# Tanh gates multiplied on VectorE, and low weight parts summed by an accumulating DMA

## The chip, the cores and the metric

The kernel runs on one NeuronCore of one Trainium2 chip. Its measure is the device time of one execution in microseconds: 2702.65 us before the change, the median of three runs (2695.49 to 2704.43).

## The reference

Two decoder layers over 1024 tokens of width 1024, in float32. A layer normalizes x and projects it by one matrix of 4352 columns into queries (16 heads of 64), keys and values (2 heads each), the convolution's value u and gate ug (512 channels each), and two output gates of 1024 channels.

```python
def conformer_conv(u, ug, w_dw, b_dw, ln_g, ln_b, w_pw):
    a = u * jax.nn.sigmoid(ug)
    y = ...causal depthwise convolution of width 31 over a, plus b_dw
    y = jax.nn.silu(layernorm(y, ln_g, ln_b))
    return y @ w_pw

h = rmsnorm(x, norm_mix[l])
q, k, v, u, ug, ga, gb = jnp.split(h @ w_in[l], SPLITS, axis=-1)
a_out = sliding_window_attention(q, k, v, sinks[l])    # QK-norm, partial rotary, window 128
c_out = conformer_conv(u, ug, ...)
merged = jax.nn.sigmoid(ga) * a_out + jax.nn.sigmoid(gb) * c_out
x = x + merged @ w_out[l]
h2 = rmsnorm(x, norm_ffn[l]); g, up = jnp.split(h2 @ w_gate_up[l], 2, axis=-1)
x = x + (jax.nn.silu(g) * up) @ w_down[l]
```

## The kernel before

Tensors lie with channels on the 128 partitions and tokens along the free axis. A float32 product is built of three matmuls: each operand is split into a high part rounded to fp32r and a low part, what is left, and high by high, high by low and low by high are summed in PSUM (`mm3`, L236).

**Weights.** `fetch` (L120) keeps a short queue of weight tiles of 128x1024. SyncE loads a tile into `raw` (L125), ScalarE rounds it into `wh` (L133), GpSimd subtracts to get `wl` (L134). There are two buffers each of `raw` and `wl` and three of `wh`, so `wl` of one tile is written while TensorE still reads that of the tile before, once TensorE has let go of the tile before that one.

**The attention stage.** After keys and values each layer runs 30 more input projections (`project`, L758; two more follow after the stage), each of eight steps of six 512-column matmuls (`dense`, L257). Between the steps TensorE does 32 attention units of two heads' two blocks each: scores `S` (`unit_s`, L625), transposes `pT` (`unit_t`), masks on GpSimd (`masks`, L678: four affine selects, `mo` twice, then `ph` and `pl` in place) and the product with the values, `po` (`unit_o`, L691), which reads all four. Before a unit's queries are used, GpSimd does their rotary products (L385, L386) and a power (L396), and SyncE copies them into `qs` (L615, L616).

VectorE runs the depthwise convolution in the same stage, as 31 taps of 128x1024 for each of four channel groups (L492, L496), between the softmax's small instructions. These taps are its largest load. The convolution's input `a` is the product of u and the sigmoid of ug, made on GpSimd (L482). The gates of branch A are multiplied with the attention's output on GpSimd (`mul_a`, L730) and stored; those of branch B are stored (L770) and multiplied later, out of PSUM, on VectorE (L811).

**Order.** TensorE's order is the program's, and in the attention stage VectorE's too: callbacks are filed on a clock that `tick` advances by one per projection step (`at`, `after`, `when_free`). `T1` and `T2` say how many steps after the scores the row maxima and the normalization follow. The orders of ScalarE, GpSimd and SyncE come from a scheduler that simulates a timeline; each engine then runs its queue strictly in order.

Of the kernel before, what the change touches and what calls it, by code (L numbers as in the profile page):

```python
# [52 lines left out]
def trunk(ctx, tc, xT, win, wcv, wout, wgu, wdn, vecs, cosT, sinT, outT):  # L53
# [63 lines left out]
    raws, ready, given = [], [], [0, 0, 0]  # L117
    part = [0]

    def fetch(limit=len(wseq)):  # L120
        limit = min(limit, wends[part[0]])
        while given[2] < limit and given[2] <= given[0] + AHEAD + 1:
            src, n = wseq[given[2]]
            raw = wp.tile([P, n], F32, tag="raw", bufs=WRAW, name="raw")
            nc.sync.dma_start(raw, src)  # L125
            raws.append(raw)
            given[2] += 1
        while given[1] < given[2] and given[1] <= given[0] + AHEAD:
            n = wseq[given[1]][1]
            raw = raws.pop(0)  # L130
            wh = wp.tile([P, n], F32R, tag="wh", bufs=WHI, name="wh")
            wl = wp.tile([P, n], F32R, tag="wl", bufs=WLO, name="wl")
            nc.scalar.copy(wh, raw)  # L133
            nc.gpsimd.tensor_tensor(out=wl, in0=raw, in1=wh.bitcast(F32), op=ALU.subtract)  # L134
            ready.append((wh, wl))
            given[1] += 1

    def next_w():
# [182 lines left out]
    for l in range(DEPTH):  # L321
# [57 lines left out]

        def rope(src):  # L380
            for h in range(2):
                o = h * HD
                nc.sync.dma_start(rot[o:o + 8], src[o + 8:o + 16])
                nc.sync.dma_start(rot[o + 8:o + 16], src[o:o + 8])
            nc.gpsimd.tensor_tensor(out=src, in0=src, in1=ct, op=ALU.mult)  # L385
            nc.gpsimd.tensor_tensor(out=rot, in0=rot, in1=st_, op=ALU.mult)  # L386

# [88 lines left out]
        def conv_g(c, ps):  # L476
            ug = t4("ug")
            nc.vector.tensor_tensor(out=ug, in0=ps, in1=R, op=ALU.mult)
            nc.scalar.activation(ug, ug, AF.Sigmoid)
            a = ap_.tile([P, T + CW - 1], F32, tag="a", bufs=2, name="a")  # L480
            nc.gpsimd.memset(a[:, 0:CW - 1], 0.0)
            nc.gpsimd.tensor_tensor(out=a[:, CW - 1:], in0=held_u.pop(c), in1=ug, op=ALU.mult)  # L482
            after(6, lambda: avals.update({c: a}))

        def conv_taps():
            for c in range(CC):
                while c not in avals:
# [93 lines left out]
        def queries(i, ps):  # L581
# [3 lines left out]
            nc.scalar.activation(sq, ps, AF.Square)  # L585
            rope(q32)
            fq = sm.tile([P, 16], F32, tag="fq", bufs=3, name="fq")
# [134 lines left out]
        def gate(ps):  # L722
            g = t4("g")
            nc.vector.tensor_tensor(out=g, in0=ps, in1=R, op=ALU.mult)  # L724
            nc.scalar.activation(g, g, AF.Sigmoid)
            return g
# [3 lines left out]
        def mul_a(i):  # L730
# [3 lines left out]
            g = gheld.pop(i)  # L734
            nc.gpsimd.tensor_tensor(out=g, in0=g, in1=Av.pop(i), op=ALU.mult)
            nc.sync.dma_start(mA[i], g)
# [17 lines left out]
        dve = ExitStack()  # L754
        dve.enter_context(tc.manual_schedule(engines={mybir.EngineType.DVE}))
        keys(psk)
        tick()
# [25 lines left out]
        while events:  # L783
            tick()
        assert conv_done[0] == CC * CW
        dve.close()
        att.close()
# [17 lines left out]
        for i in range(8):  # L805
# [4 lines left out]
            ps = dense(zs, True)  # L810
            nc.vector.tensor_tensor(out=gb, in0=ps, in1=gb, op=ALU.mult)  # L811
            nc.vector.tensor_tensor(out=gb, in0=gb, in1=ga, op=ALU.add)
# [15 lines left out]
        for e in range(KD):  # L828
            nc.sync.dma_start(xacc[e], xT[e] if l == 0 else xnx[e])
            ps = dense(ms, True)  # L830
            if e >= KD - 3:
                ahead(2 * (e - KD + 4))
            nc.vector.tensor_tensor(out=xacc[e], in0=xacc[e], in1=ps, op=ALU.add)
            nc.sync.dma_start(xsp[e], xacc[e])
# [313 lines left out]
TAIL = 2  # L1148
T1, T2, SCB = 2.2, 3.5, 2
QSP = 7  # L1150
# [7 lines left out]
QSB = 4  # L1158
WRAW, WHI, WLO, T4 = 2, 3, 2, 4


# [61 lines left out]
```

## Time and profile before

| what | value |
|---|---|
| profiled execution: time, span | 2704.77 us, 2703.0 us |
| median of the three runs | 2702.65 us |
| busy: TensorE, VectorE, ScalarE, GpSimd | 2588.6, 1843.6, 1190.6, 1601.5 us |
| mean granted TensorE clock | 0.975 |
| busy in taps (L496), 240 instructions | 402.6 us |
| busy in weight subtractions (L134), 100 instructions | 241.0 us |
| issued by DMA queues of SyncE and ScalarE | 393.63 and 0.09 MB |

In the wait lists, "A <- B" means that A's engine sat idle until B's instruction released it. In the group lists a row gives source line, engine, operation, out<-in, shape and count, then busy us and mean ns of one, then the idle time before them and its releasers. L numbers are lines of the kernel before.

### The profile page before, as it was taken

The numbers are of one execution on the slowest core, as the hardware profiler recorded it, in microseconds if no ns is written. First come the engines' busy times: TensorE is split into PE (matmuls) and PEld (weight loads), VectorE is DVE, ScalarE is ACT, GpSimd is POOL, SyncE is SP. The second block draws the span as 40 slices with busy tenths as digits, with TensorE's granted clock in tenths as the row PEclk, the third lists the DMA queues.
The fourth block names the chain that finished last, engine by engine and source line by source line (L and its number), as shares of the span: only waits on it lengthen the run. The fifth ranks groups of instructions, "written<-read, shape, count | busy, mean of one in ns | idle before, by whom it ended". The sixth has DMA issues, their size and how long they took to land.

```text
span 2703.0 us, 33316 instructions
## 1 busy us (share of the span) xinstructions
PE 2588.6 (96%) x11736; PEld 2118.2 (78%) x11736; DVE 1843.6 (68%) x2037; ACT 1190.6 (44%) x2299; POOL 1601.5 (59%) x1028
## 2 busy tenths in 40 slices
PE   7999999999999999999999999989999999999999
PEld 5777777788787888878777777778887788888887
DVE  6689998552567777845637899895616678778344
ACT  2266666742432323344523566668425222223443
POOL 7368776525256767765534777775252677767544
PEclk8999999999999999999999999989999999999999
DMA  3222222475244454476721222234752444455666
GB/s 129 57 66 58 82 80 67 158 271 208 90 164 147 168 179 156 160 269 218 238 67 52 65 88 65 74 93 156 252 203 94 179 168 146 162 179 193 223 223 210
DMA packets 137478, 395.83 MB, mean 146 GB/s; under 512 B 16160, under 2 KB 16416, under 8 KB 137312
## 3 DMA queue, kind: packets, MB, share of 16 engines
q1 hardware_dynamic: 137168, 393.63, 43.3%
q8 instruction: 92, 1.51, 0.2%
q14 instruction: 74, 0.61, 0.1%
q10 hardware_dynamic: 144, 0.09, 0.0%
HBM read 259.17 MB, written 115.34 MB: 139 GB/s over the span
## 4 chain that ended last, share of the span: by engine, by line
PE 64%; DVE 21%; DMA 4%; POOL 4%; issue 3%; ACT 2%; SPq 1%; DVEq 0%; ACTq 0%; POOLq 0%
PE b L850 40%; PE ps L242 20%; DVE y L496 9%; DVE mx L652 1%; DVE sc L648 1%; DVE q L610 1%; DVE acc L295 1%; DVE A L714 1%; DMA qs<-q 1%; PE po L702 1%; POOL q L385 1%; DVE pl L679 1%; DVE g L724 1%; DMA x<-xs 1%; POOL wl L134 1%
## 5 line engine op out<-in xcount | busy, mean ns | idle before, releaser
L151 POOL TENSOR_TENSOR plo<-fraw,phi 128x512 fp32r<-128x512 f32 x290 | 421.4, 1461 | 232.5 <-ACT phi L149 217.4
L134 POOL TENSOR_TENSOR wl<-raw,wh 128x1024 fp32r<-128x1024 f32 (+1 forms) x100 | 241.0, 2411 | 292.2 <-PE ps L242 250.3
L151 POOL TENSOR_TENSOR plo<-fs,phi 128x512 fp32r<-128x512 f32 x160 | 264.7, 1665 | 252.0 <-ACT phi L149 240.4
L496 DVE SCALAR_TENSOR_TENSOR y<-a,vec,y 128x1024 f32<-128x1024 f32 x240 | 402.6, 1678 | 3.6
L149 ACT CAST phi<-fraw 128x512 fp32r<-128x512 f32 x444 | 257.6, 618 | 246.7 <-POOL plo L151 133.6
L242 PE MATMUL ps<-hx,wh 128*128 128x512 f32 x1056 | 350.6, 414 | 7.2 <-ACT hx L283 7.2
L242 PE MATMUL ps<-lx,wh 128*128 128x512 f32 x1056 | 341.0, 405 | 0.8 <-DVE lx L284 0.8
L242 PE MATMUL ps<-hx,wl 128*128 128x512 f32 x1056 | 337.4, 401 | 4.5 <-POOL wl L134 4.5
L149 ACT CAST phi<-fs 128x512 fp32r<-128x512 f32 x160 | 95.4, 620 | 533.9 <-DVE fs L164 520.1
L151 DVE TENSOR_TENSOR plo<-fraw,phi 128x512 fp32r<-128x512 f32 x154 | 129.8, 848 | 191.5 <-ACT phi L149 189.3
L242 PEld LDWEIGHTS ps<-hx,wl 128*128 128x128 f32 x1056 | 206.7, 196 | 50.8 <-POOL wl L134 4.9
L850 PE MATMUL b<-plo,phi 128*128 128x512 f32 x616 | 241.1, 391 | 4.5 <-DVE plo L151 4.2
L242 PEld LDWEIGHTS ps<-lx,wh 128*128 128x128 f32 x1056 | 207.6, 197 | 48.3 <-DVE lx L284 1.5
L850 PE MATMUL b<-phi,plo 128*128 128x512 f32 x616 | 240.4, 390 | 0.0
L850 PE MATMUL b<-phi 128*128 128x512 f32 x616 | 240.4, 390 | 0.0
L242 PEld LDWEIGHTS ps<-hx,wh 128*128 128x128 f32 x1056 | 196.1, 198 | 43.1 <-ACT hx L283 7.2
L133 ACT CAST wh<-raw 128x1024 fp32r<-128x1024 f32 (+1 forms) x100 | 98.1, 981 | 175.7 <-PE ps L242 137.1
L656 ACT ACTIVATE sc<-sc,nm,fq 128x129 f32<-128x129 f32 x256 | 123.8, 486 | 70.4 <-DVE nm L654 69.9
L918 POOL TENSOR_TENSOR g<-g,u 128x512 f32<-128x512 f32 (+1 forms) x84 | 129.3, 1557 | 31.6 <-DVE u L971 25.2
L914 DVE TENSOR_TENSOR g<-g 128x512 f32<-128x512 f32 x88 | 103.9, 1181 | 62.8 <-POOL g L918 42.5
L850 PEld LDWEIGHTS b<-plo,phi 128*128 128x128 f32 x616 | 116.1, 188 | 31.8 <-DVE plo L151 7.8
L850 PEld LDWEIGHTS b<-phi 128*128 128x128 f32 x616 | 116.0, 188 | 24.3
(254 smaller groups left out, 6141.2 us busy)
## 6 DMA issues: line engine op xcount, KB each, us to landing
fraw<-wgu SPq DMA_DIRECT2D x88, 512.0 KB
raw<-win SPq DMA_DIRECT2D x68, 512.0 KB
act<-g SPq DMA_DIRECT2D x44, 512.0 KB
dw<-wdn SPq DMA_DIRECT2D x44, 512.0 KB
td<-g SPq DMA_DIRECT2D x44, 512.0 KB
sd<-dw SPq DMA_DIRECT2D x44, 512.0 KB
fraw<-sd SPq DMA_DIRECT2D x88, 256.0 KB
fraw<-td SPq DMA_DIRECT2D x88, 256.0 KB
```

The costliest lines, as they stand in the source:

```text
L133: nc.scalar.copy(wh, raw)
L134: nc.gpsimd.tensor_tensor(out=wl, in0=raw, in1=wh.bitcast(F32), op=ALU.subtract)
L149: nc.scalar.copy(hi, src)
L151: (eng or nc.gpsimd).tensor_tensor(out=lo, in0=src, in1=hi.bitcast(F32), op=ALU.subtract)
L242: nc.tensor.matmul(ps[:, sl], a[:, wc], b[:, sl], start=first and j == 0, stop=last and j == 2)
L295: (add or nc.gpsimd).tensor_tensor(out=acc, in0=acc, in1=sq, op=ALU.add)
L385: nc.gpsimd.tensor_tensor(out=src, in0=src, in1=ct, op=ALU.mult)
L496: nc.vector.scalar_tensor_tensor(out=y, in0=a[:, j:j + T], scalar=V(w0 + j), in1=y, op0=ALU.mult, op1=ALU.add)
L656: nc.scalar.activation(sc[:, n], sc[:, n], AF.Exp, bias=nm[:, n:n + 1], scale=fq[:, 4 * j + n:4 * j + n + 1], accum_out=den[:, n:n + 1])
L850: nc.tensor.matmul(ps, w[:, ai * P:(ai + 1) * P], x, start=first and j == 0, stop=last and j == 2, skip_group_check=True)
L914: nc.vector.tensor_tensor(out=o, in0=x, in1=y, op=ALU.subtract)
L918: nc.gpsimd.tensor_tensor(out=g[:, sl], in0=g[:, sl], in1=u[:, sl], op=ALU.mult)
```

## The change

Four things. A gate's sigmoid becomes tanh of half its argument, since sigmoid(x) = (1 + tanh(x/2)) / 2; each product with a gate becomes (t + 1) times the other factor by one `scalar_tensor_tensor` on VectorE, and the missing halves go into the tap weights (one 128x124 instruction per layer) and into the addition to x. The convolution's input and branch A's product thereby move from GpSimd to VectorE. In the attention stage alone (`spaced`) a weight's low part is made by ScalarE writing the negative of the high part and a DMA on GpSimd's queue adding the weight from HBM onto it; 60 of the 100 weight tiles are made so. `T2` goes from 3.5 to 4.2. `rope` gets a parameter, given as 0, by which it stays as it was.

```diff
--- before.py
+++ after.py
@@ -116,6 +116,7 @@
         wends.append(len(wseq))
     raws, ready, given = [], [], [0, 0, 0]
     part = [0]
+    spaced = [False]
 
     def fetch(limit=len(wseq)):
         limit = min(limit, wends[part[0]])
@@ -126,14 +127,22 @@
             raws.append(raw)
             given[2] += 1
         while given[1] < given[2] and given[1] <= given[0] + AHEAD:
-            n = wseq[given[1]][1]
+            src, n = wseq[given[1]]
             raw = raws.pop(0)
             wh = wp.tile([P, n], F32R, tag="wh", bufs=WHI, name="wh")
             wl = wp.tile([P, n], F32R, tag="wl", bufs=WLO, name="wl")
             nc.scalar.copy(wh, raw)
-            nc.gpsimd.tensor_tensor(out=wl, in0=raw, in1=wh.bitcast(F32), op=ALU.subtract)
+            low(wl, raw, wh, src)
             ready.append((wh, wl))
             given[1] += 1
+
+    def low(wl, raw, wh, src):
+        if not spaced[0]:
+            nc.gpsimd.tensor_tensor(out=wl, in0=raw, in1=wh.bitcast(F32), op=ALU.subtract)
+            return
+
+        nc.scalar.activation(wl, wh.bitcast(F32), AF.Copy, scale=-1.0)
+        nc.gpsimd.dma_start(wl, src, accum_op=ALU.add)
 
     def next_w():
         fetch()
@@ -377,13 +386,16 @@
         def inproj():
             return dense(xs)
 
-        def rope(src):
+        now = lambda n, fn: fn()
+
+        def rope(src, later=0):
             for h in range(2):
                 o = h * HD
                 nc.sync.dma_start(rot[o:o + 8], src[o + 8:o + 16])
                 nc.sync.dma_start(rot[o + 8:o + 16], src[o:o + 8])
-            nc.gpsimd.tensor_tensor(out=src, in0=src, in1=ct, op=ALU.mult)
-            nc.gpsimd.tensor_tensor(out=rot, in0=rot, in1=st_, op=ALU.mult)
+            eng = nc.vector if later else nc.gpsimd
+            (after if later else now)(later, lambda: eng.tensor_tensor(out=src, in0=src, in1=ct, op=ALU.mult))
+            (after if later else now)(later + 1, lambda: eng.tensor_tensor(out=rot, in0=rot, in1=st_, op=ALU.mult))
 
         def headnorm(sq, f):
             pss = ps_o("pssh")
@@ -476,13 +488,20 @@
         def conv_g(c, ps):
             ug = t4("ug")
             nc.vector.tensor_tensor(out=ug, in0=ps, in1=R, op=ALU.mult)
-            nc.scalar.activation(ug, ug, AF.Sigmoid)
+            nc.scalar.activation(ug, ug, AF.Tanh, scale=0.5)
             a = ap_.tile([P, T + CW - 1], F32, tag="a", bufs=2, name="a")
             nc.gpsimd.memset(a[:, 0:CW - 1], 0.0)
-            nc.gpsimd.tensor_tensor(out=a[:, CW - 1:], in0=held_u.pop(c), in1=ug, op=ALU.mult)
-            after(6, lambda: avals.update({c: a}))
+
+            def product():
+                nc.vector.scalar_tensor_tensor(out=a[:, CW - 1:], in0=ug, scalar=1.0, in1=held_u.pop(c),
+                                               op0=ALU.add, op1=ALU.mult)
+                avals[c] = a
+            after(1.5, product)
 
         def conv_taps():
+
+            nc.vector.tensor_scalar(out=V(V_CWT, CC * CW), in0=V(V_CWT, CC * CW), scalar1=0.5, scalar2=None,
+                                    op0=ALU.mult)
             for c in range(CC):
                 while c not in avals:
                     yield 0
@@ -583,7 +602,7 @@
             nc.scalar.activation(q32, ps, AF.Copy, scale=V(V_GQ))
             sq = t4("sqh")
             nc.scalar.activation(sq, ps, AF.Square)
-            rope(q32)
+            rope(q32, RD)
             fq = sm.tile([P, 16], F32, tag="fq", bufs=3, name="fq")
             nfq = sm.tile([P, 16], F32, tag="nfq", bufs=3, name="nfq")
             sr = sm.tile([P, NB, 2], F32, tag="sr", bufs=3, name="sr")
@@ -722,7 +741,7 @@
         def gate(ps):
             g = t4("g")
             nc.vector.tensor_tensor(out=g, in0=ps, in1=R, op=ALU.mult)
-            nc.scalar.activation(g, g, AF.Sigmoid)
+            nc.scalar.activation(g, g, AF.Tanh, scale=0.5)
             return g
 
         done_o = set()
@@ -732,7 +751,8 @@
                 after(1, lambda: mul_a(i))
                 return
             g = gheld.pop(i)
-            nc.gpsimd.tensor_tensor(out=g, in0=g, in1=Av.pop(i), op=ALU.mult)
+            nc.vector.scalar_tensor_tensor(out=g, in0=g, scalar=1.0, in1=Av.pop(i),
+                                           op0=ALU.add, op1=ALU.mult)
             nc.sync.dma_start(mA[i], g)
 
 
@@ -753,6 +773,7 @@
         after(0 if l else NA, norm_a)
         dve = ExitStack()
         dve.enter_context(tc.manual_schedule(engines={mybir.EngineType.DVE}))
+        spaced[0] = True
         keys(psk)
         tick()
         def project(j):
@@ -783,6 +804,7 @@
         while events:
             tick()
         assert conv_done[0] == CC * CW
+        spaced[0] = False
         dve.close()
         att.close()
 
@@ -808,7 +830,7 @@
             gb = zp.tile([P, T], F32, tag="gb", bufs=3, name="gb")
             nc.sync.dma_start(gb, sB[i])
             ps = dense(zs, True)
-            nc.vector.tensor_tensor(out=gb, in0=ps, in1=gb, op=ALU.mult)
+            nc.vector.scalar_tensor_tensor(out=gb, in0=gb, scalar=1.0, in1=ps, op0=ALU.add, op1=ALU.mult)
             nc.vector.tensor_tensor(out=gb, in0=gb, in1=ga, op=ALU.add)
             ms.append(split_plain(gb, f"m{i}"))
         zp_s.close()
@@ -830,7 +852,8 @@
             ps = dense(ms, True)
             if e >= KD - 3:
                 ahead(2 * (e - KD + 4))
-            nc.vector.tensor_tensor(out=xacc[e], in0=xacc[e], in1=ps, op=ALU.add)
+            nc.vector.scalar_tensor_tensor(out=xacc[e], in0=ps, scalar=0.5, in1=xacc[e],
+                                           op0=ALU.mult, op1=ALU.add)
             nc.sync.dma_start(xsp[e], xacc[e])
             tick()
         rgt.close()
@@ -1146,7 +1169,7 @@
 S0 = 16
 SP = 6.0
 TAIL = 2
-T1, T2, SCB = 2.2, 3.5, 2
+T1, T2, SCB = 2.2, 4.2, 2
 QSP = 7
 TS = 1.42
 LN1 = 7
@@ -1157,6 +1180,7 @@
 QN = 5
 QSB = 4
 WRAW, WHI, WLO, T4 = 2, 3, 2, 4
+WD, RD = 2, 0
 
 
 def _tables():
```

GpSimd's queue in layer 0, at the rotary products of one set of queries, before: rotary products (q, rot), power (fq), masks (mo, ph, pl), weight split (wl), convolution input (a), channel sum (lsum).

```order
L385 TENSOR_TENSOR q_2745<-q_2745,ct 128x1024
L386 TENSOR_TENSOR rot<-rot,st__202 128x1024
L396 TENSOR_TENSOR fq<-ssb,mhalf 128x16
L684 AFFINE_SELECT mo<-ph 128x512
L684 AFFINE_SELECT mo<-pl 128x512
L134 TENSOR_TENSOR wl<-raw,wh 128x1024
L687 AFFINE_SELECT ph<-ph 128x512
L687 AFFINE_SELECT pl<-pl 128x512
L482 TENSOR_TENSOR a<-ur,ug 128x1024
L502 TENSOR_TENSOR lsum<-lsum,y 128x1024
```

The same stretch after (GpSimd, with the masks of a unit before it):

```order
L145 DMA wl<-win 128x1024
L706 AFFINE_SELECT pl<-pl 128x512
L397 TENSOR_TENSOR q_2767<-q_2767,ct 128x1024
L398 TENSOR_TENSOR rot<-rot,st__202 128x1024
L408 TENSOR_TENSOR fq<-ssb,mhalf 128x16
L521 TENSOR_TENSOR lsum<-lsum,y 128x1024
L703 AFFINE_SELECT mo<-ph 128x512
L703 AFFINE_SELECT mo<-pl 128x512
L706 AFFINE_SELECT ph<-ph 128x512
L145 DMA wl<-win 128x1024
L706 AFFINE_SELECT pl<-pl 128x512
```

The subtraction is gone from ahead of both in-place masks; a DMA issue stands between them, and the channel sum now stands ahead of the four masks. At one other set of queries of this layer it stands ahead of the power.

One projection later in the queue, where no channel sum is near, at the next set of queries, GpSimd's queue before:

```order
L385 TENSOR_TENSOR q_3205<-q_3205,ct 128x1024
L386 TENSOR_TENSOR rot<-rot,st__202 128x1024
L396 TENSOR_TENSOR fq<-ssb,mhalf 128x16
L684 AFFINE_SELECT mo<-ph 128x512
L684 AFFINE_SELECT mo<-pl 128x512
L134 TENSOR_TENSOR wl<-raw,wh 128x1024
L687 AFFINE_SELECT ph<-ph 128x512
L687 AFFINE_SELECT pl<-pl 128x512
```

The split stands between the first and the second pair of masks; and after:

```order
L397 TENSOR_TENSOR q_3230<-q_3230,ct 128x1024
L398 TENSOR_TENSOR rot<-rot,st__202 128x1024
L408 TENSOR_TENSOR fq<-ssb,mhalf 128x16
L703 AFFINE_SELECT mo<-ph 128x512
L703 AFFINE_SELECT mo<-pl 128x512
L706 AFFINE_SELECT ph<-ph 128x512
L706 AFFINE_SELECT pl<-pl 128x512
L145 DMA wl<-win 128x1024
```

Here the masks follow each other and the DMA issue follows them.

ScalarE's queue in layer 0 around the second convolution gate (ug) after the units began, before:

```order
L133 CAST wh<-raw 128x1024
L607 CAST qhi<-q_1372 128x1024
L663 ACTIVATE sc<-sc,ri 128x128 x4
L479 ACT_TABLE_LOAD
L479 ACTIVATE ug<-ug 128x1024
L641 COPY sc<-S 128x4x128
L639 COPY sc<-sr 128x4
L674 CAST ph<-pT 128x512
L707 COPY sh<-po 64x256
L708 COPY sh<-po 64x256
L656 ACT_TABLE_LOAD
L656 ACTIVATE sc,den<-sc,nm,fq 128x129 x4
```

and after:

```order
L626 CAST qhi<-q_1384 128x1024
L134 CAST wh<-raw 128x1024
L144 ACTIVATE wl<-wh 128x1024
L491 ACTIVATE ug<-ug 128x1024
L682 ACTIVATE sc<-sc,ri 128x128 x4
L660 COPY sc<-S 128x4x128
L658 COPY sc<-sr 128x4
L693 CAST ph<-pT 128x512
L726 COPY sh<-po 64x256
L727 COPY sh<-po 64x256
L675 ACTIVATE sc,den<-sc,nm,fq 128x129 x4
```

Both table loads are gone (73 on this queue before, 4 after), and the negation (wl<-wh) follows the weight's rounding.

On VectorE a product stands among the taps, three or four instructions behind the scaling of its gate, and the reciprocals (L661) come somewhat later among them; TensorE's order changes only near the end of each stage, where one scores unit and two small matmuls of the convolution's normalization change places with projection steps.

## Rows read from the trace of the kernel before

**Rows 1.** The two attention stages: length, busy time per engine, granted clock, DMA.

```profile
100.00:500.00 400.00, 366.74 (x1802) 303.69 (x1801) 354.37 (x390) 240.72 (x575) 277.50 (x173) 0.94 0.26 77
1430.00:1860.00 430.00, 395.28 (x1947) 327.60 (x1946) 373.10 (x413) 259.72 (x611) 287.98 (x181) 0.94 0.27 82
```

**Rows 2.** Who TensorE waited for, 100 to 500 us: total, times, longest.

```profile
PE po L702 <- POOL ph L687: 9.2, 4, 3.0
PE S L636 <- DMA qs<-q: 6.3, 6, 2.2
PE po L702 <- DVE ssb L394: 5.7, 3, 2.2
PE po L702 <- POOL pl L687: 4.3, 4, 1.2
```

**Rows 3.** The same wait list of SyncE's DMA queue, whole execution.

```profile
SPq L125 <- POOL wl L134: 459.0, 71, 21.0
```

**Rows 4.** Groups by line, 100 to 500 us: count, busy us, mean ns, idle before.

```profile
L496 DVE SCALAR_TENSOR_TENSOR y<-a,vec,y 128x1024 f32<-128x1024 f32 x116 | 195.4, 1684 | 1.7
L610 DVE TENSOR_TENSOR q<-q,qhi 128x1024 fp32r<-128x1024 f32 x8 | 21.4, 2672 | 0.0
L134 POOL TENSOR_TENSOR wl<-raw,wh 128x1024 fp32r<-128x1024 f32 x23 | 62.8, 2730 | 25.6 <-PE ps L242 25.4 <-POOL mo L684 0.2
L385 POOL TENSOR_TENSOR q<-q,ct 128x1024 f32<-128x1024 f32 x8 | 25.5, 3193 | 16.0 <-DMA rot<-q 16.0
L386 POOL TENSOR_TENSOR rot<-rot,st__202 128x1024 f32<-128x1024 f32 x8 | 25.0, 3129 | 0.0
L735 POOL TENSOR_TENSOR g<-g,A 128x1024 f32<-128x1024 f32 x6 | 16.6, 2772 | 4.4 <-ACT g L725 2.3 <-ACT sc L639 2.1
L482 POOL TENSOR_TENSOR a<-ur,ug 128x1024 f32<-128x1024 f32 x3 | 9.2, 3052 | 0.0
L502 POOL TENSOR_TENSOR lsum<-lsum,y 128x1024 f32<-128x1024 f32 x3 | 7.1, 2376 | 0.0
L656 ACT ACT_TABLE_LOAD x13 | 16.7, 1283 | 6.6 <-DVE nm L654 6.4
L133 ACT CAST wh<-raw 128x1024 fp32r<-128x1024 f32 x23 | 24.1, 1050 | 5.6 <-PE ps L242 5.2 <-issue 0.3
```

**Rows 5.** Timeline of layer 0, VectorE beside GpSimd: start, duration, instruction.

```profile
212.13 1.22 DVE L478 TENSOR_TENSOR ug<-ps,R 128x1024 f32<-128x1024 f32 x1
213.27 1.28 DVE L496 SCALAR_TENSOR_TENSOR y<-a,vec,y 128x1024 f32<-128x1024 f32 x1
216.78 3.37 POOL L482 TENSOR_TENSOR a<-ur,ug 128x1024 f32<-128x1024 f32 x1
217.82 3.41 DVE L496 SCALAR_TENSOR_TENSOR y<-a,vec,y 128x1024 f32<-128x1024 f32 x1
```

**Rows 6.** Timeline of layer 0, a weight split ahead of two masks.

```profile
369.45 2.35 POOL L134 TENSOR_TENSOR wl<-raw,wh 128x1024 fp32r<-128x1024 f32 x1
371.75 1.62 POOL L687 TENSOR_SCALAR_AFFINE_SELECT ph<-ph 128x512 fp32r<-128x512 f32 x1
373.43 0.58 PE L702 MATMUL po<-ph,vv 128*128 128x256 f32 x1 [3.01 <-POOL ph L687]
375.00 0.58 PE L702 MATMUL po<-pl,vv 128*128 128x256 f32 x1 [0.99 <-POOL pl L687]
376.23 1.05 PE L242 MATMUL ps<-hx,wh 128*128 128x512 f32 x2
380.38 0.63 PE L242 MATMUL ps<-hx,wl 128*128 128x512 f32 x2
```

**Rows 7.** Chain that ended last, layer 0: start, duration, what.

```profile
166.34 6.30 DMA qs<-q
180.54 3.81 DMA yd<-y
547.89 12.28 PE ps L242 x54
```

## The prediction

> **What bounds the kernel now.** I read the table by stage first, then TensorE's waits, the groups by line of one attention stage, and last two stretches of the timeline. The attention stages [rows 1] run from 100 to 500 us and from 1430 to 1860 us. In the first TensorE is busy 366.74 of 400 us, so it idles 33.3 us, and in the second 430 - 395.28 = 34.7 us. The granted clock in both is 0.94, a mixture of TensorE's two levels, 2.4 and 1.2 GHz. A shortfall of 6% over 830 us is 50 us of lost work. Idle time and lost clock together are 68 + 50 = 118 us, and this is the most that a change confined to these stages can give back unless it takes work from TensorE, which this one does not.
>
> VectorE is busy 354.37 of the first 400 us, GpSimd 277.50, ScalarE 240.72 [rows 1]. TensorE waits there for GpSimd's masks (9.2 and 4.3 us), for query copies by DMA (6.3), and for VectorE to release PSUM (5.7) [rows 2]. So the stage is paced by VectorE and GpSimd, not by TensorE's own work.
>
> These two disturb each other. A tap that starts while GpSimd is idle takes 1.28 us; one that starts inside a GpSimd product takes 3.41 us, and the GpSimd product beside it 3.37 us [rows 5]. On average a tap took 1.684 us [rows 4], so VectorE's busy time holds waiting: 116 x (1.684 - 1.28) = 46.9 us in taps, and 8 x (2.672 - 1.28) = 11.1 us in query splits (L610). That is 58 us in one stage.
>
> **GpSimd's share.** In the first stage it does 51 products or sums of two 128x1024 tiles: weight splits 62.8 us, rotary products 25.5 + 25.0, gate products 16.6, convolution inputs 9.2, channel sums 7.1; 146.2 us together [rows 4]. The change removes weight splits, gate products and convolution inputs, 88.6 us or 61%. Of VectorE's 58 us of waiting, 61% is 35 us if these products cause all of it, and about 18 us if the small masks cause half. VectorE gains nine products, 3 + 6, in the same window. The trace has no such instruction with this scalar, but the same operation and shape is the tap, 1.28 us [rows 5], so 9 x 1.28 = 11.5 us. The net relief is between 6 and 24 us. I take 20, near the upper end: the jump from 1.28 to 3.41 us under a single product, 2.1 us each time, is large enough for 51 of them to explain all 58 us. TensorE follows VectorE where VectorE is the pace; by its busy share, 354 / 400, I count 18 of the 20 us.
>
> **GpSimd ahead of TensorE.** At 369.45 us a weight split of 2.35 us starts ahead of two in-place masks, and TensorE waits 3.01 and then 0.99 us for them. Afterwards a pair of matmuls takes 1.05 us from 376.23 on, and again 0.63 by 380.38 us: the clock is at its lower level after the wait, and some 4 us at half speed cost about 1.8 us more [rows 6]. Four such waits make up the 9.2 us [rows 2]. In the new queue the split is gone, but at two of the four places the channel sum, 7.1 / 3 = 2.4 us [rows 4], has moved ahead of the masks and keeps them as late. At the other two I count 2.35 us and half of the clock's 1.8, so 2 x 3.25 = 6.5, rounded to 6 us.
>
> **ScalarE.** It gains a negation for each weight, which nothing in the trace shows; the nearest row is the cast of the same tile, 1.050 us [rows 4], so 23 x 1.05 = 24 us per stage. It loses its table loads, 16.7 us ahead of the exponentials alone [rows 4]. The engine was idle 159 us of the stage [rows 1]. I count nothing, but the negation must wait until TensorE lets go of the `wl` buffer, and it stands in order on ScalarE, with softmax exponentials and PSUM copies behind it. Formerly GpSimd did that waiting. This could cost a stall or save one; it belongs to the range.
>
> **Accumulating DMA.** No transfer of before adds onto its destination, and none was issued from GpSimd's queue. A `wl` buffer is released when one projection ends and is needed when the next has ended. There are 23 splits in 400 us [rows 4], a period of 17.4 us; without attention units 54 matmuls took 12.28 us, so a projection of 48 takes 10.9 [rows 7]. Into this slack must fit the negation, the issue and the transfer. Storing 512 KB took 3.81 us on the chain [rows 7]. At best, with nothing for the issue, the path is 1.05 + 3.81 = 4.9 us. At worst the transfer takes twice the longest copy on the chain, 2 x 6.30 = 12.6 us [rows 7], behind one GpSimd instruction of 3.4 us [rows 5]: 1.05 + 3.4 + 12.6 = 17.1 us. I take 8 us, nearer the lower end since the 512 KB transfer is the nearest row; the rest of the period covers it, and the cost is nothing. Were it as long as the worst, the projections that have no units beside them would each wait 17.1 - 10.9 = 6.2 us; in the new queue six issues per layer stand ahead of the first mask.
>
> Two further effects help and are not in the sum. The `raw` buffer is now freed by the cast and not by the split, while SyncE's queue waited 459.0 us in total for splits before it could load the next weight [rows 3], with the query copies queued behind that load.
>
> The Trainium skill speaks against this DMA ("SBUF — State Buffer", section "SBUF: two separate sides"): a DMA issued from GpSimd has its descriptors written by GpSimd, and while VectorE runs an instruction in a two-port mode these cannot be written; a copy of about 620 ns took about 3100 ns. By that page an issue could be some 2.5 us longer, an estimate, and my path 10.5 us in place of 8: the sum stays, but the rival of the late weight gains a chance, which I put at 0.16 where the rows alone would have me say 0.11. No row before shows a DMA on that queue.
>
> **Other edits.** Gates of branch B and the addition to x change their form, 16 instructions each over both layers, reading PSUM. A PSUM read of this shape takes 1.22 us and a tap 1.28 [rows 5], so 32 x 0.06 = 2 us on VectorE, outside the attention stages where TensorE's own work covers it. If it were not covered, it would cost these 2 us. The scaling of the tap weights is one small instruction per layer. The later normalization (`T2`) lets taps run ahead of the reciprocal; whether it gains or loses a microsecond per unit is not to be seen in the trace.
>
> **Sum.** Per layer 18 + 6 = 24 us, for two layers 48 us. Against the profiled execution, 2704.77 us, that is 2656.8; the median of the runs lies 2.1 us lower, which gives 2655 us.
>
> **Rivals.**
> - The weight comes late. The accumulating path is at its upper bound of 17.1 us, and TensorE waits for `wl`: 2 x 6 x 6.2 = 74 us more. Minus 48 this is +26, or 2729 us. It decides from a path of 10.9 + 48 / 12 = 14.9 us on; below that the change still gains. For it speaks that every transfer crosses HBM and then SBUF twice and that the issue stands in order behind masks; against it that projections with units have 17.4 us.
> - VectorE takes back what it got. The small masks cause half of the waiting, the net relief is 6 us per layer and the masks are as late as before: 2702.65 - 12 = 2691 us. For it speaks that VectorE's load hardly changes; against it the length of a tap under a product [rows 5].
> - All stalls go and the clock stays at its upper level: 2702.65 - 118 = 2585 us. For it speaks that the lower level follows waits [rows 6], so that fewer waits pay twice; against it that rotary products, power and half of VectorE's load remain.
>
> **How the numbers follow.** I give the forecast 0.52, the late weight 0.16, the taking back 0.19, and the vanishing stalls 0.13. The range runs from 2600 to 2715 us: below it lies most of the third rival's mass, above it most of the first's. A difference of 0.3%, about 8 us, is what a measurement of this kernel can tell from none. The second rival straddles that border, half in half. So faster is 0.52 + 0.13 + 0.10 = 0.75, same 0.09, slower 0.16.
>
> **What would show it.** After the change taps should average 1.4 to 1.55 us in place of 1.684, and TensorE's idle time in each attention stage should fall to 15 to 25 us with a clock of 0.96 or more. TensorE's waits for the accumulating DMA should be few and below 2 us. ScalarE's table loads should have gone except one or two per layer. The prediction is wrong if TensorE waits for `wl` or ScalarE sits long before the negation, if taps stay at 1.65 us or more, or if the masks come no earlier because the DMA issue itself holds GpSimd for as long as the split did.

## The result and the profile after

The changed kernel takes 2659.01 us (median of four runs, 2657.32 to 2660.84). The kernel before, run beside it, takes 2700.11 (four runs, 2695.49 to 2704.43). The ratio is 0.9853 [0.9838, 0.9868]: 41 us less, where 2655 us was forecast. The profiled execution takes 2658.14 us, its span is 2656.4 us, and its mean granted clock 0.987 in place of 0.975.

The stage windows of after, in the columns of [rows 1]; the second window lies 30 us earlier, since layer 1 now starts earlier:

```profile
100.00:500.00 400.00, 375.40 (x1898) 310.33 (x1897) 334.90 (x418) 246.57 (x614) 215.25 (x174) 0.97 0.48 121
1400.00:1830.00 430.00, 404.12 (x2050) 334.25 (x2049) 354.07 (x438) 261.26 (x644) 220.35 (x181) 0.98 0.48 120
```

TensorE idles 400 - 375.40 = 24.6 us in the first and 25.9 us in the second, against 33.3 and 34.7 before. In the same 400 us it gets through 1898 matmuls in place of 1802. Both windows gain by this count 5.3%, 21 and 23 us, which is nearly all of the 46.6 us between the two profiled executions. The work that follows the stage agrees: its second pair of matmuls of the gates of branch B starts at 549.1 us in place of 571.3 in layer 0, so that 22 us are gained by then, and 47 where these gates end in layer 1 (1909.2 against 1956.4).

One matmul is busy 375.40 / 1898 = 197.8 ns on average, before 366.74 / 1802 = 203.5. Over 1898 matmuls of about the same mixture this is some 11 us, a little more than the 8.7 us of idle time. In the second stage it is 197.1 ns in place of 203.0, 12.1 us over 2050 matmuls, beside 8.8 us of idle time. By this estimate the higher granted clock (0.97 and 0.98 for 0.94) gives 23 us and the shorter waits 17.5.

TensorE's waits from 95 to 480 us, to hold against [rows 2] (total us, times, longest):

```profile
PE S L655 <- DVE sc L667: 8.5, 3, 6.7
PE S L655 <- DMA qs<-q: 6.7, 5, 2.3
PE pT L691 <- ACT sc L682: 4.5, 6, 1.3
PE po L721 <- DVE ssb L406: 1.9, 2, 1.0
PE po L721 <- POOL pl L706: 1.0, 1, 1.0
PE po L721 <- POOL mo L703: 0.9, 1, 0.9
PE po L721 <- POOL ph L706: 0.7, 1, 0.7
```

The masks cost 2.6 us where they cost 13.5. No row names the accumulating DMA. The groups of 100 to 480 us answer to [rows 4], which go to 500 us:

```profile
L515 DVE SCALAR_TENSOR_TENSOR y<-a,vec,y 128x1024 f32<-128x1024 f32 x113 | 167.8, 1485 | 1.7
...
L144 ACT ACTIVATE wl<-wh 128x1024 fp32r<-128x1024 f32 x23 | 24.3, 1055 | 0.1
L134 ACT CAST wh<-raw 128x1024 fp32r<-128x1024 f32 x23 | 24.1, 1046 | 2.3 <-PE ps L251 2.0
...
L145 POOL DMA_DIRECT2D wl<-win x23 | 20.3, 884 | 48.3 <-ACT wl L144 45.2 <-ACT sc L658 3.1
...
L629 DVE TENSOR_TENSOR q<-q,qhi 128x1024 fp32r<-128x1024 f32 x8 | 11.6, 1448 | 0.0
```

Taps fell from 1684 to 1485 ns, query splits from 2672 to 1448. The negation takes 1055 ns and is ready to run when its turn comes (0.1 us idle ahead of 23). GpSimd still stands ahead of each weight, longer than before: 48.3 us ahead of the issues, 45.2 of them for the negation, where it stood 25.6 ahead of the splits [rows 4]. The masks behind that wait are late for only 2.6 us.

The page's list of DMA issues gives the median time from issue to landing:

```profile
wl<-win POOLq DMA_DIRECT2D x60, 512.0 KB, 6.4
```

What got worse is seen in the timeline of layer 0, at the change from one channel group to the next (start, duration, instruction; idle time before it in brackets):

```profile
249.95 0.92 POOL L145 DMA_DIRECT2D wl<-win  x1
...
254.01 0.73 SPq L522 DMA_DIRECT2D yd<-y  x1
...
263.06 0.81 DVE L511 TENSOR_SCALAR y<-a,vec 128x1024 f32<-128x1024 f32 x1 [8.07 <-DMA yd<-y]
...
265.88 0.47 PE L655 MATMUL S<-kh,qs 128*128 128x128 f32 x1 [6.74 <-DVE sc L667]
```

The tile `y` has one buffer, so the next group's first tap (L511) waits until `y` is stored. The store is issued at 254.01, behind query copies and another store, and lands 9 us later, while transfers of weights are under way. VectorE stands 8.07 us, and the score copy (L667) behind it keeps TensorE for 6.74 us. On the chain of before such a store took 3.81 us [rows 7]. Not every store is so slow in after: the first of the layer is faster than that, 2.7 us.

```profile
164.71 0.33 SPq L522 DMA_DIRECT2D yd<-y  x1
...
167.41 0.81 DVE L511 TENSOR_SCALAR y<-a,vec 128x1024 f32<-128x1024 f32 x1 [1.74 <-DMA yd<-y]
```

Over the whole execution, before and after:

```profile
DVE ri L661 <- ACT sc L656: 35.3, 20, 2.6
...
PE po L702 <- POOL ph L687: 18.4, 8, 3.0
...
DVE y L492 <- DMA yd<-y: 7.8, 2, 3.9
PE pT L672 <- ACT sc L663: 5.1, 9, 1.1
```

```profile
DVE ri L680 <- ACT sc L675: 20.4, 13, 3.7
DVE y L511 <- DMA yd<-y: 18.3, 4, 8.1
...
PE pT L691 <- ACT sc L682: 9.6, 13, 1.3
```

VectorE waits 15 us less for the sums of the exponentials (L680, the reciprocal) and 10.5 us more for the store. But its whole idle time ahead of a group's first tap did not grow, as the group rows of the two executions show:

```profile
L492 DVE TENSOR_SCALAR y<-a,vec 128x1024 f32<-128x1024 f32 x8 | 7.2, 896 | 21.1 <-POOL a L482 8.3 <-DMA yd<-y 7.8 <-POOL lsum L502 5.0
```

```profile
L511 DVE TENSOR_SCALAR y<-a,vec 128x1024 f32<-128x1024 f32 x8 | 6.8, 846 | 18.5 <-DMA yd<-y 18.3
```

Before, it stood there 21.1 us for GpSimd's product and channel sum and for the store; after, 18.5 us for the store. In gates_only below, which has the moved products but not the added DMAs, it waits 11.8 us for the store. The DMA engines' share in the stage went from 0.26 [rows 1] to 0.48, the bytes moved from 77 to 121 GB/s.

### The profile page after: what moved, and what is told of

Same layout as the page of the kernel before. It is cut to its first block, busy times and chain, and to the rows that moved or that the text cites. A ratio compares the mean times of both kernels' runs of the same rounds, so it can differ in the third digit from the quotient of the medians.

```text
span 2656.4 us, 33362 instructions
## 1 busy us (share of the span) xinstructions
PE 2562.6 (96%) x11736; PEld 2094.6 (79%) x11736; DVE 1785.8 (67%) x2063; ACT 1152.9 (43%) x2290; POOL 1423.7 (54%) x1004
## 4 chain that ended last, share of the span: by engine, by line
PE 69%; DVE 13%; DMA 6%; ACT 4%; issue 3%; POOL 3%; SPq 1%; DVEq 0%; ACTq 0%; POOLq 0%
PE b L873 43%; PE ps L251 21%; DVE y L515 5%; DMA qs<-q 2%; DMA rot<-q 1%; PE po L721 1%; POOL rot L398 1%; PE pT L691 1%; ACT wh L134 1%; DVE q L412 1%; DVE acc L304 1%; POOL q L397 1%; DMA yd<-y 1%; DVE A L733 1%; DVE mx L671 1%
## 5 line engine op out<-in xcount | busy, mean ns | idle before, releaser
L515 DVE SCALAR_TENSOR_TENSOR y<-a,vec,y 128x1024 f32<-128x1024 f32 x240 | 358.4, 1493 | 3.8
L251 PE MATMUL ps<-hx,wh 128*128 128x512 f32 x1056 | 343.2, 406 | 7.2 <-ACT hx L292 7.2
L251 PE MATMUL ps<-hx,wl 128*128 128x512 f32 x1056 | 331.9, 395 | 6.0 <-POOL wl L141 6.0
L251 PE MATMUL ps<-lx,wh 128*128 128x512 f32 x1056 | 332.7, 396 | 0.8 <-DVE lx L293 0.8
L141 POOL TENSOR_TENSOR wl<-raw,wh 128x1024 fp32r<-128x1024 f32 (+1 forms) x40 | 79.9, 1998 | 192.7 <-PE ps L251 176.4
L145 POOL DMA_DIRECT2D wl<-win x60 | 53.3, 888 | 177.6 <-ACT wl L144 172.6
L706 POOL TENSOR_SCALAR_AFFINE_SELECT ph<-ph 128x512 fp32r<-128x512 f32 x64 | 69.3, 1083 | 143.0 <-DVE pl L698 143.0
```

The lines of the kernel that those rows point to most:

```text
L145: nc.gpsimd.dma_start(wl, src, accum_op=ALU.add)
L251: nc.tensor.matmul(ps[:, sl], a[:, wc], b[:, sl], start=first and j == 0, stop=last and j == 2)
L515: nc.vector.scalar_tensor_tensor(out=y, in0=a[:, j:j + T], scalar=V(w0 + j), in1=y, op0=ALU.mult, op1=ALU.add)
L706: nc.gpsimd.affine_select(out=src, in_=src.bitcast(F32), pattern=[[0, 4], [-1, P]], compare_op=ALU.is_gt, fill=0.0, base=0, channel_multip ...
```

## The experiments

My theory was the prediction's: the gain comes from GpSimd's products that are gone, by shorter taps and earlier masks. The rivals gave it to the steps that I had costed at nothing: the table loads, `T2`, the DMA traffic. Differences between variants are of medians; taken instead by each variant's ratio to the kernel before beside it, they shift by up to some 5 us.

**Gates without the DMA** (gates_only). The low parts stay with GpSimd:

```diff
-        spaced[0] = True
```

> The changed kernel, but every low weight part is subtracted on GpSimd as before; gates by tanh and their products on VectorE stay. Theory (the gain comes from the 128x1024 two-input instructions that leave GpSimd, of whose time in a stage 62.8 of 88.6 us were weight splits): VectorE's relief from the 25.8 us of gate and convolution products, 58 x 25.8 / 146 = 10 us per stage, is eaten by the 11.5 us of products it takes over; between 2690 and 2702 us, taps at 1.60 us or more. Rival (the gain comes from the gates: no table loads on ScalarE, products no longer behind masks on GpSimd): 2680 us or less.

2684.0 us (2682.6 to 2684.94), 0.9930 [0.9914, 0.9947]. It fell between the two. Over the whole run TensorE waits 9.0 us for `ph`, half of before's 18.4, and taps take 1534 ns. It is no faster than the kernel before with `T2` alone (2681.57, below): without the DMA, tanh and the products on VectorE bring nothing that can be seen.

**The DMA alone** (dma_only). Before, with `low` and `spaced` and nothing else:

```diff
+        nc.scalar.activation(wl, wh.bitcast(F32), AF.Copy, scale=-1.0)
+        nc.gpsimd.dma_start(wl, src, accum_op=ALU.add)
```

> The kernel before with the accumulating DMA alone: sigmoid, its table loads and the products on GpSimd stay. Theory: the weight splits are most of it, relief 58 x 62.8 / 146 = 25 us per stage on VectorE and none given back; 2650 to 2668 us, taps at 1.45 to 1.55 us. Rival (ScalarE, with the negations added and the table loads kept, holds up the softmax): 2680 us or more, with TensorE's waits for ScalarE's normalization (4.5 us in a stage of the changed kernel) doubled.

2670.9 us (2666.74 to 2671.5), 0.9879 [0.9865, 0.9894]: 3 us above the theory's range and far from the rival's. It is the largest single part, 31 us of saving by medians of one batch. TensorE's waits for masks are gone (0.6 us in all), its waits for query copies have grown from 9.5 to 29.4 us, and taps take 1575 ns. Its first stage (columns of [rows 1]; the profiled execution took 2666.74 us):

```profile
100.00:500.00 400.00, 368.44 (x1889) 306.44 (x1888) 340.67 (x411) 280.11 (x639) 225.82 (x182) 0.98 0.48 120
```

TensorE idles 31.6 us, hardly less than before's 33.3, but one matmul takes 195.0 ns in place of 203.5, which is 16 us over 1889: here the gain is nearly all granted clock (0.98 for 0.94).

**Sigmoid kept, products on VectorE** (sigmoid_dve). After, with the table loads back (the halves go as well, and the product of branch B and the addition to x are again as before):

```diff
-            nc.scalar.activation(g, g, AF.Tanh, scale=0.5)
+            nc.scalar.activation(g, g, AF.Sigmoid)
...
-            nc.vector.scalar_tensor_tensor(out=g, in0=g, scalar=1.0, in1=Av.pop(i),
-                                           op0=ALU.add, op1=ALU.mult)
+            nc.vector.tensor_tensor(out=g, in0=g, in1=Av.pop(i), op=ALU.mult)
```

> The changed kernel with sigmoid in place of tanh and plain products on VectorE, so that the table loads (73 instead of 4) come back while everything else stays. Theory (ScalarE had 159 idle us of 400 in a stage): 2659 to 2666 us. Rival (with the negation and the cast of a weight in front, each pair of table loads, 2.6 us, shows in TensorE's wait for normalized scores): 24 gates at 1 us or more each, 2680 us or more.

2686.91 us (2684.17 to 2689.77), 0.9942 [0.9927, 0.9957], 28 us more than after. The rival was right: I had counted nothing for ScalarE. Waits over the whole execution:

```profile
PE pT L688 <- ACT sc L679: 32.5, 21, 2.4
...
PE S L652 <- DVE sc L664: 20.0, 10, 5.4
```

TensorE waits 32.5 us for normalized scores, where after waits 9.6. The taps are as short as after's, 1482 ns over the execution, and the time is 28 us longer: short taps alone do not make the gain.

**T2 put back** (t2_back). After with one constant changed:

```diff
-T1, T2, SCB = 2.2, 4.2, 2
+T1, T2, SCB = 2.2, 3.5, 2
```

> The changed kernel with T2 at 3.5 again. Theory (the place of the reciprocal among the taps is worth little): 2655 to 2664 us. Rival (it had to be moved, since VectorE otherwise waits for the exponentials behind ScalarE's longer queue): VectorE's wait at the reciprocal grows from nothing to some 15 us in a stage, 2675 us or more.

2690.03 us (2683.96 to 2693.51), 0.9951 [0.9936, 0.9967], 31 us more than after. Again the rival's time came true; VectorE's wait at the reciprocal grew from 20.4 us, not from nothing, and by 17 us in both stages together, about half of what the rival said. Waits, whole execution:

```profile
DVE ri L680 <- ACT sc L675: 37.4, 24, 4.5
...
PE po L721 <- DVE ssb L406: 25.2, 12, 4.4
```

VectorE runs its queue in order. A reciprocal filed early waits there for the exponentials, and behind it stands the copy (L406) for which TensorE waits, 25.2 us in place of 6.7. Between the two stand three taps, and at the longest waits it is their length that counts. Two such places of layer 0:

```profile
192.66 0.18 DVE L680 RECIPROCAL ri<-den 128x4 f32<-128x4 f32 x1 [4.53 <-ACT sc L675]
192.76 3.89 DVE L515 SCALAR_TENSOR_TENSOR y<-a,vec,y 128x1024 f32<-128x1024 f32 x3
...
197.01 0.71 PE L721 MATMUL po<-mo,vv 128*128 128x256 f32 x4 [0.16 <-DVE ssb L406]
...
241.85 0.18 DVE L680 RECIPROCAL ri<-den 128x4 f32<-128x4 f32 x1 [1.49 <-ACT sc L675]
241.95 7.89 DVE L515 SCALAR_TENSOR_TENSOR y<-a,vec,y 128x1024 f32<-128x1024 f32 x3
242.81 2.67 POOL L397 TENSOR_TENSOR q<-q,ct 128x1024 f32<-128x1024 f32 x1 [0.66 <-DMA rot<-q]
245.44 3.32 POOL L398 TENSOR_TENSOR rot<-rot,st__202 128x1024 f32<-128x1024 f32 x1
...
250.19 0.70 PE L721 MATMUL po<-mo,vv 128*128 128x256 f32 x4 [4.14 <-DVE ssb L406]
```

At the first the reciprocal waits 4.53 us, the three taps take 3.89 and TensorE waits 0.16. At the second it waits 1.49 us, but the taps take 7.89 beside GpSimd's rotary products, and TensorE waits 4.14. The other three waits of 4 us for this copy also have three taps of some 8 us ahead of them.

**T2 alone** (before_t2). The same constant in before, 3.5 to 4.2.

> The kernel before with T2 at 4.2 alone. Theory (the later reciprocal pays only where ScalarE's queue makes the exponentials late, as the change does): within 8 us of before, 2694 to 2710 us. Rival (the later reciprocal is worth 31 us by itself, the difference seen between T2 3.5 and 4.2 in the changed kernel): 2670 to 2680 us, with VectorE's wait at the reciprocal, 35.3 us in both layers, halved.

2681.57 us (2679.28 to 2690.14), 0.9936 [0.9920, 0.9953]. The theory was wrong, the rival near. The waits are those of the profiled execution, the slowest of the four (2690.14 us). The reciprocal's wait falls from 35.3 to 16.1 us, and with it TensorE's waits for `ph`, from 18.4 to 2.8:

```profile
PE pT L672 <- ACT sc L663: 25.4, 23, 2.1
DVE ri L661 <- ACT sc L656: 16.1, 10, 2.6
...
PE po L702 <- POOL ph L687: 2.8, 4, 0.9
```

With sigmoid's loads still on ScalarE the later normalization reaches TensorE late instead (25.4 us). Taps stay at 1672 ns (1678 before): 18 us without any shorter tap.

**T2 later still** (t2_46). After with 4.6:

> The changed kernel with T2 at 4.6. Theory (TensorE then waits for the normalization instead, since the transposes' place is unchanged): VectorE's wait at the reciprocal falls below 15 us in both layers and TensorE's wait for normalized scores rises above 15 from 9.6; 2655 to 2675 us. Rival (the time moves by some 20 us with any small change of order, since other queues are ordered anew): 2675 us or more with neither wait changed so.

2659.43 us (2658.81 to 2662.15), 0.9859 [0.9844, 0.9873], the same as after. The wait of the reciprocal falls to 10.9 us, and that of TensorE for the scores rises to 27.3. Taps take 1445 ns, 48 less than after's 1493 over the execution, and nothing comes of it.

**Tanh, products left on GpSimd** (tanh_pool, tanh_pool_t2). Dma_only with the tanh activation, at `T2` 3.5 and 4.2:

```diff
-            nc.scalar.activation(g, g, AF.Sigmoid)
+            nc.scalar.activation(g, g, AF.Tanh, scale=0.5)
```

> The kernel of dma_only with tanh of half the argument in place of sigmoid, products on GpSimd as before and nothing else; it leaves out the addition of one and the halves, so its gates are not sigmoids. It takes away the table loads alone, 69 x 1.28 = 88 us of ScalarE's time. Theory (table loads are hidden where the products are not on VectorE's queue): 2660 to 2671 us, dma_only's 2671 or little below. Rival (table loads cost what they did beside the products on VectorE, 28 us): 2640 to 2650 us.

2656.59 us (2653.11 to 2660.07), 0.9846 [0.9832, 0.9861], between the two expectations. That is 14 us less than dma_only with sigmoid (9 by the ratios), though taps take 1593 ns.

> The kernel of tanh_pool (accumulating DMA, tanh, products left on GpSimd; the addition of one and the halves are left out) with T2 at 4.2. Beside the changed kernel it differs only in where the products are made. Theory (the move of the products to VectorE costs time at either T2, 33 us at 3.5 by t2_back against tanh_pool): the later reciprocal gives its 18 us here too, 2632 to 2645 us. Rival (at 4.2 it is all the same where the products are made): 2654 to 2664 us.

2656.41 us (2654.02 to 2658.18), 0.9843 [0.9828, 0.9858]; the rival was right, and `T2` is worth nothing here, although VectorE's wait at the reciprocal halves and taps shorten to 1498 ns. Waits of the whole execution at 3.5, then at 4.2:

```profile
DVE ri L670 <- ACT sc L665: 35.9, 26, 3.2
...
PE po L711 <- DVE ssb L403: 12.6, 8, 4.1
```

```profile
DVE ri L670 <- ACT sc L665: 16.5, 14, 2.3
...
PE pT L681 <- ACT sc L672: 12.3, 14, 1.9
...
PE ps L251 <- DMA wl<-win: 7.3, 2, 4.0
```

At 4.2 TensorE's wait for the copy is down to 0.8 us and that for query copies from 29.7 to 21.3. In their place it waits 12.3 us for normalized scores (1.6 at 3.5) and, twice, for the accumulating DMA. With the accumulating DMA and tanh throughout, the four corners are (those on GpSimd leave out the addition of one and the halves):

| products on | T2 = 3.5 | T2 = 4.2 |
|---|---|---|
| GpSimd | 2656.6 | 2656.4 |
| VectorE | 2690.0 | 2659.0 |

Moving the products to VectorE gains nothing in either column, and at the old `T2` it costs 33 us.

**A DMA that doesn't add** (plain_dma):

```diff
-        nc.gpsimd.dma_start(wl, src, accum_op=ALU.add)
+        nc.gpsimd.dma_start(wl, src)
```

> The changed kernel with plain DMAs on GpSimd's queue in place of the accumulating ones: the low part is then overwritten by the weight itself, so its values are wrong, and no addition and no read of the destination remain. Theory (the transfer's 6.4 us are covered): landing at 4 to 5.5 us, and 2650 to 2662 us, within 8 us of the changed kernel. Rival (the addition holds the DMA engines and with them the stores and query copies that TensorE waits for): 2645 us or less.

2650.95 us (2646.75 to 2652.55), 0.9825 [0.9809, 0.9842]; the theory held, at its lower edge. The page's row:

```profile
wl<-win POOLq DMA_DIRECT2D x60, 512.0 KB, 5.1
```

Adding costs 1.3 us of each transfer, and the DMA share of the first stage is 0.42 without it and 0.48 with it at nearly the same 123 and 121 GB/s. The issue holds GpSimd for 582 ns on average without it and 888 with it. In all it costs about 8 us, which is at the edge of what these runs can tell from none.

**Rotary products on VectorE too** (rope_dve):

```diff
-WD, RD = 2, 0
+WD, RD = 2, 2
```

> The changed kernel with the queries' rotary products on VectorE (RD = 2) in place of GpSimd. Theory by the prediction's main term (what counts is how long taps wait for GpSimd's two-input instructions): 50 us of these leave GpSimd per stage, taps fall to 1.40 us or less, VectorE gains 16 x 1.28 = 20 us; net a gain of 10 us or more, 2650 us or less. Rival (tap length and time go apart, as in t2_46 and tanh_pool; VectorE's order and its waits decide): 2662 us or more in spite of short taps.

2680.88 us (2673.92 to 2693.09, six runs), 0.9938 [0.9919, 0.9958]: 22 us more than after, with the shortest taps of all, 1349 ns. Waits, whole execution:

```profile
DVE q L397 <- DMA rot<-q: 60.3, 16, 7.4
...
PE po L721 <- DVE ssb L406: 28.5, 14, 2.3
```

In after GpSimd's queue takes this wait for a DMA (25.9 us), and TensorE waits only 3.8 us for masks; in VectorE's queue the copy (L406) stands behind it, for which TensorE waits 28.5 us. So the run does not show what fewer GpSimd products are worth by themselves: a later place for these products might do better. That was not tried.

**Two buffers of y** (y2). To make room, `wh` goes from three buffers to two:

```diff
-                y = ap_.tile([P, T], F32, tag="y", bufs=1, name="y")
+                y = ap_.tile([P, T], F32, tag="y", bufs=2, name="y")
...
-WRAW, WHI, WLO, T4 = 2, 3, 2, 4
+WRAW, WHI, WLO, T4 = 2, 2, 2, 4
```

> The changed kernel with two buffers of the convolution's sum y, and two of the high weight part in place of three to make room. In the changed kernel VectorE waited 18.3 us in both layers for the store of y to land before the next group's first tap, and TensorE 6.7 us once behind that. Theory: these waits go, 2640 to 2652 us. Rival (VectorE uses the time up elsewhere, or the missing third buffer makes ScalarE wait for TensorE): 2655 us or more.

2646.51 us (2645.14 to 2652.21), 0.9813 [0.9798, 0.9828], the fastest measured, 12.5 us below after and 53 below the runs of before beside it. Its stages (columns of [rows 1]):

```profile
100.00:500.00 400.00, 380.39 (x1947) 314.06 (x1946) 338.52 (x426) 253.79 (x633) 219.66 (x179) 0.99 0.49 124
1400.00:1830.00 430.00, 405.21 (x2082) 334.76 (x2081) 355.36 (x438) 269.30 (x652) 226.67 (x185) 1.00 0.50 125
```

VectorE's wait for the store is gone, TensorE's wait for the score copy falls from 14.2 to 3.7 us, and the granted clock is 0.99 and 1.00. Taps are a little longer than after's, 1507 ns. The other buffer count changed with it and was not separated.

**The same, attention units starting one step later** (y2_s17): `S0` 16 to 17.

> The kernel of y2 with S0 at 17, so that every attention unit starts one projection step, 1.4 us, later against its queries. In y2 TensorE still waited 16.2 us in both layers for query copies by DMA. Theory (these waits are lateness, and a step covers most of each): 13 waits of 1.2 us fall below 4 us in total and the time to 2634 to 2642 us. Rival (the whole stage is paced by VectorE and ScalarE, whose order only shifts along): 2644 us or more.

2660.53 us (2658.98 to 2665.27), 0.9855 [0.9837, 0.9873], 14 us more than y2. The wait for query copies fell from 16.2 to 6.0 us as hoped, and the masks' came back:

```profile
PE po L721 <- POOL pl L706: 16.4, 14, 1.8
...
PE po L721 <- POOL ph L706: 10.2, 6, 3.1
```

The rival's time came true, by another cause than it named.

## Why the prediction was right, and where it was not

The direction, the place and the size held: 41 us measured, 48 forecast, all made in the two attention stages. Its signs came too, but for one that was just missed: taps between 1.4 and 1.55 us (1.485), idle time of 15 to 25 us per stage (24.6, but 25.9 in the second), a clock of 0.96 or more (0.97, 0.98), no wait for the accumulating DMA, and ScalarE's 73 loads down to 4.

- **The accumulating DMA.** I took 8 us for the path and no wait for it. Measured are 1.055 for the negation, and 6.4 us from the issue to landing, so 7.5 us behind a free GpSimd. TensorE never waits for it in after; in tanh_pool_t2 it does twice, 7.3 us in all. The rival of the late weight did not come about, and the Trainium skill's warning ("SBUF — State Buffer", section "SBUF: two separate sides") did not show here: the 60 issues take 888 ns on average, none over 1.1 us, while VectorE is busy 84% of the stage. The Trainium skill speaks there of VectorE's two-port modes, and no run shows whether the instructions here run in one. Dma_only shows the DMA to be the largest single part, 31 us.
- **The masks.** I expected two of four places to stay late. They came in time at nearly all, 2.6 us of waiting in place of 13.5. Over the execution TensorE's waits for `ph` and `pl`, 27.3 us before, are 2.9 in after, 11.8 with `T2` alone and 0.6 with the DMA alone. There the waits for query copies grew by 19.9 us in their place, so the masks' 27 us are not all gain.
- **VectorE's relief, the main term, was not borne out.** "TensorE follows VectorE where VectorE is the pace", 18 us per layer, turned nine tenths of the relief into time. The taps did shrink as forecast, but mean length and time come apart: 1445 ns at 2659.4 us, 1349 at 2680.9, 1482 at 2686.9, 1593 at 2656.6, 1672 at 2681.6. From tanh_pool to tanh_pool_t2 the taps lose 23 us of VectorE's time, and the kernel's stays as it is. A stretched tap costs TensorE time where it stands ahead of an instruction that TensorE waits for, as the two places in t2_back show. How much of the DMA's 31 us came through shorter taps was not separated.
- **`T2`, costed at nothing, was mis-sized.** The prediction said that its worth "is not to be seen in the trace". The wait list of before had the row: 35.3 us of VectorE waiting at the reciprocal (L661). `T2` is worth 18 us in before, 31 in after, and nothing with the DMA, tanh and the products on GpSimd: its worth hangs on what else stands in the queues.
- **The table loads, costed at nothing too.** Beside the DMA they are worth 14 us with products on GpSimd (dma_only against tanh_pool) and 28 with products on VectorE (sigmoid_dve against after). In the second pair ScalarE's idle time in the stage didn't cover them: TensorE's wait for normalized scores, which come from ScalarE's queue, grew from 9.6 to 32.5 us. In the first pair it grew from 1.6 to 5.5 only, so the 14 us are not explained by it.
- **Products on VectorE** were counted as part of the gain. By the table of four they bring none; without the later `T2` they cost 33 us.
- **The clock was mis-sized.** It was in the sum with under 2 us per layer. By the mean matmul it gave 10.9 us in the first stage and 12.1 in the second, more than the idle time that went, and in the first stage of dma_only nearly all of the gain. What the DMA does that lets the clock rise so far was not separated.
- **The `raw` buffer**, freed earlier, was named as help outside the sum. SyncE's queue waited 505.0 us for ScalarE's casts before it could load the next weight, where it waited 459.0 for the splits [rows 3], and TensorE's waits for query copies went from 9.5 to 14.4 us. No help is to be seen.
- **The store of y** was not in the prediction. VectorE waits 18.3 us for it, 6.5 more than in gates_only without the added DMAs; but in before it had stood as long at the same place, for other instructions. Y2 took the wait away and 12.5 us with it.

So that the total came so near was luck: the sum left out the table loads, `T2` and nearly all of the clock, and counted a relief of VectorE that the runs do not bear out. Step by step the 41 us come apart in two ways. With the DMA first, it saves 31 us and tanh 14; `T2` and then the products on VectorE change nothing clear (0 and 3 us more). With `T2` first, it saves 18 us, tanh and the products change nothing clear (2 us more), and the DMA saves 25. On both ways the DMA is the largest part. The parts do not add: the DMA alone saves 31 us and the gates with `T2` alone 18, together 49, while both together save 41. Why the overlap is 8 us was not settled. Each edit lets the scheduler reorder ScalarE's, GpSimd's and SyncE's queues, so no variant changes one thing only. A kernel that alters only how VectorE and GpSimd disturb each other was not built.

## What to carry to other kernels

Before costing an edit by an instruction's duration, look in the wait lists of the in-order engines for the instruction at which a queue stands, and ask who waits behind it: moving one such instruction (`T2`) was worth 31 us, 18 us or nothing here, depending on what else stood in the queues, and taking nine products per stage off GpSimd by putting them on VectorE was worth nothing. Look for single buffers whose release is a DMA: such a wait can stand hidden behind others until these go. A second buffer of y, with one buffer less of the high weight part, gave 12.5 us here. Before blaming a wait on a change, add up all that the engine waited for at that instruction before. Test the parts of a bundle by themselves and in pairs: the products' move was harmless only with its neighbour.

## What the hardware showed that was not expected

- Adding onto the destination makes a 512 KB transfer from GpSimd's queue land in 6.4 us, in place of 5.1 (medians of 60), and raises the DMA share from 0.42 to 0.48 at like throughput.
- Issuing such a DMA holds GpSimd for 888 ns on average (582 without the adding), against 2730 ns for the subtraction that it replaces [rows 4].
- A 512 KB store that took 3.81 us [rows 7] before took, in one execution of after, 2.7 us (164.71 to 167.41) at one place and 9 us amid other transfers (254.01 to 263.06) at another.
- Three taps in a row took 3.89 us at one place of t2_back and 7.89 beside two of GpSimd's products at another.
